# A batched matmul of fp32 inputs: releasing the first of sixteen output stores one load earlier

## The chip, the cores and the metric

The kernel runs on one core of a Trainium2 chip. The metric is the device time of one execution in microseconds (us), as the median of several runs. The times inside an execution come from one profiled execution of each kernel. In the profile PE is TensorE, PEld its weight loads, DVE is VectorE, ACT ScalarE, POOL GpSimd, SP SyncE; a trailing q (SPq) is that engine's sequencer.

## The reference

```python
# batch, m, k, n = 16, 512, 512, 512; a and b are float32
def reference(a, b):
    return np.matmul(a, b.transpose(0, 2, 1)).astype(np.float32)
```

The inputs are 33.55 MB and the output is 16.78 MB, so 50.33 MB cross between memory and the core's on-chip buffer.

## The kernel before

The work goes in eight pairs of matrices. Pair u is fed by load 2u (two matrices of a, 2.10 MB) and load 2u+1 (two of b), and it makes outputs 2u and 2u+1, each stored by one transfer of 1.05 MB. VectorE casts each load to bf16, TensorE transposes it and multiplies, ScalarE copies transposed a's and the results out of PSUM, the memory that TensorE writes. Seven slots hold loads (NL) and seven hold outputs (NO). All loads but one and the last eight stores are issued by SyncE into one queue; the first eight stores are issued by GpSimd into another one. A store in GpSimd's queue can therefore share the transfer engines with the loads; a store in SyncE's queue stands behind all the loads that were issued before it (store 8, issued by SyncE at 73.36 us, landed at 104.66, after load 15 at 99.49).

```python
NL = 7
NO = 7
STORES = "SSSSOSOSOSSOOOOOO"               # GpSimd: S issues a store, O frees an output slot
LATE = {11: (8, 9), 13: (10, 11), 15: (12, 13)}   # SyncE: stores issued after load n landed
# ... (buffers, semaphores)

def load(n, engine=nc.sync):
    u, slot = n // 2, n % NL
    # ... (source address)
    if n >= NL:
        nc.sync.wait_ge(s_cd, n - NL + 2)          # the slot has been cast
    engine.dma_start(ld[:, slot], src).then_inc(s_ld[slot], 16)

# ... (landed(n): the semaphore of store n, and 16)

def store(n):
    engine = nc.gpsimd if n < STORES.count("S") else nc.sync
    engine.wait_ge(s_out, n + 1)                   # output n is copied
    engine.dma_start(
        out[n].rearrange("(p j) n -> p j n", j=J), ob[:, n % NO]
    ).then_inc(s_st[n], 16)

load(0)
load(1, nc.scalar)
for n in range(2, NL):
    load(n)
for n in range(2 * pairs):
    nc.sync.wait_ge(s_ld[n % NL], 16 * (n // NL + 1)).then_inc(s_go, 1)
    if n > 0 and n + NL - 1 < 2 * pairs:
        load(n + NL - 1)
    for m in LATE.get(n, ()):
        store(m)
store(batch - 2)
store(batch - 1)
# ...
n_st = n_of = 0
nc.gpsimd.wait_ge(s_ld[0], 32)                     # slot 0 filled twice: load 7 has landed
for what in STORES:
    if what == "S":
        store(n_st)
        n_st += 1
    else:
        nc.gpsimd.wait_ge(*landed(n_of)).then_inc(s_of, 1)
        n_of += 1
# ... (VectorE; ScalarE takes one s_of before it writes an output, seven are given at the start;
#      TensorE)
```

## Time and profile before

| | before |
|---|---|
| time, median of the first three runs | 125.56 us (125.42 to 125.84) |
| span in the profile | 123.7 us |
| mean transfer rate over the span | 407 GB/s |
| load 7, load 15 landed | 42.26, 99.49 us |
| last store issued, landed | 113.69, 122.26 us |

The lines are shown with the prediction. Three things matter when reading them. The page's DMA row gives the busy tenths of the 16 transfer engines in 40 slices of about 3.1 us, and the GB/s row what they moved. The table by stretches counts a packet's bytes where the packet starts, so a stretch of 2 us is rough by some per cent. A line of a timeline ends, in brackets, with the idle time of the engine before it and what ended it. The landing times come from the trace's completion records: the last of 16 engines counts.

### The profile page before, as it was taken

What the parts mean: (1) busy time and instruction counts of PE and PEld (TensorE: products, weight loads), DVE (VectorE), ACT (ScalarE), POOL (GpSimd) and SP (SyncE); (2) the same over time, 40 slices, a digit from 0 to 9 for tenths busy, and PEclk for the clock granted to TensorE, in tenths of its full rate; (3) what the DMA queues carried; (4) which work ended last, traced back from release to release, by engine and by line L of the source; (5) the groups of instructions that cost most, each with busy time, mean ns of one, the idle gap of its engine ahead of it and who ended that gap; (6) DMA issues with size and microseconds to landing.
All of it is one profiled execution on the core that took longest, in us unless ns stands there. A gap on an engine that the chain in (4) does not pass through costs nothing. (4 is left out here: it accounts for less than half of the span.)

```text
span 123.7 us, 2364 instructions
## 1 busy us (share of the span) xinstructions
PE 90.8 (73%) x768; PEld 55.9 (45%) x768; DVE 68.1 (55%) x96; ACT 68.0 (55%) x130; POOL 5.2 (4%) x14
## 2 busy tenths in 40 slices
PE   0000189999999899989998999999899919995000
PEld 0000177447644754674476347645754528441000
DVE  0000698983895689289918974865957078400000
ACT  4000065478855956795589369765946069655000
POOL 2000000000000250001010110000000000000000
PEclk9999999999999999999999999999999986999955
DMA  4999999999999999999999999999999999999990
GB/s 148 413 435 429 429 429 424 429 424 435 435 424 424 429 392 363 445 416 424 453 405 437 443 408 443 424 424 458 397 445 427 408 429 427 429 427 429 424 387 8
DMA packets 4608, 50.33 MB, mean 407 GB/s; under 512 B 512, under 2 KB 512, under 8 KB 512
## 3 DMA queue, kind: packets, MB, share of 16 engines
q1 hardware_dynamic: 3312, 39.85, 76.2%
q0 software_dynamic: 1152, 8.39, 16.1%
q10 hardware_dynamic: 144, 2.10, 4.2%
HBM read 33.55 MB, written 16.78 MB: 407 GB/s over the span
## 5 line engine op out<-in xcount | busy, mean ns | idle before, releaser
L249 PE MATMUL ps<-tb,ta 128*128 128x512 bf16 x256 | 57.8, 379 | 0.5
L207 ACT COPY ob<-ps 128x512 f32 x64 | 34.4, 589 | 29.2 <-PE ps L249 21.3
L189 ACT COPY ta<-tp 128x512 bf16<-128x512 bf16 x64 | 32.9, 610 | 15.0 <-PE tp L230 15.0
L249 PEld LDWEIGHTS ps<-tb,ta 128*128 128x128 bf16 x256 | 24.1, 98 | 30.6 <-issue 4.0
L230 PE MATMUL tp<-ident,ha 128*128 128x128 bf16 x256 | 19.3, 228 | 18.1 <-PEq L135 18.1
L230 PEld LDWEIGHTS tp<-ident,ha 128*128 128x128 bf16 x256 | 16.3, 102 | 21.9 <-issue 20.1
L170 DVE COPY tb<-tp 128x1024 bf16<-128x1024 bf16 x32 | 21.2, 684 | 4.2 <-DVEq L135 4.2
L230 PE MATMUL tp<-ident,hb 128*128 128x128 bf16 x256 | 18.5, 230 | 3.4 <-PEq L135 3.4
L230 PEld LDWEIGHTS tp<-ident,hb 128*128 128x128 bf16 x256 | 16.3, 103 | 4.0 <-issue 4.0
L154 DVE CAST ha<-ld 128x1024 bf16 x8 | 5.5, 687 | 14.3 <-DVEq L135 14.3
L165 DVE COPY ha<-wa 128x2048 bf16<-128x2048 bf16 x8 | 5.5, 691 | 12.7 <-DVEq L135 12.7
L160 DVE CAST wa<-ld 128x2048 bf16 x8 | 9.8, 1220 | 0.0
L160 DVE CAST wb<-ld 128x2048 bf16 x8 | 9.7, 1217 | 0.0
L154 DVE CAST hb<-ld 128x1024 bf16 x8 | 5.5, 692 | 7.3 <-DVEq L135 7.3
L103 POOL DMA_DIRECT2D out_dram<-ob x8 | 4.5, 570 | 65.5 <-DMA ld<-in_b_dram 40.9
L169 DVE COPY hb<-wb 128x2048 bf16<-128x2048 bf16 x8 | 5.5, 685 | 0.1
L157 DVE CAST ha<-ld 128x1024 bf16 x8 | 5.5, 686 | 0.0
L157 DVE CAST hb<-ld 128x1024 bf16 x8 | 5.5, 686 | 0.0
L180 ACT ACT_TABLE_LOAD x1 | 1.3, 1283 | 1.5 <-SPq L43 1.5
L79 POOL TENSOR_SCALAR_AFFINE_SELECT ident<-ident 128x128 bf16<-128x128 bf16 x1 | 0.3, 283 | 0.2 <-POOL ident L77 0.2
L77 POOL MEMSET ident<- 128x128 bf16 x1 | 0.2, 204 | 0.5 <-SPq L43 0.5
L180 ACT COPY one<-const-float32-1.0 128x1 f32<-128x1 f32 x1 | 0.2, 192 | 0.0
(4 smaller groups left out, 0.4 us busy)
## 6 DMA issues: line engine op xcount, KB each, us to landing
ld<-in_a_dram SPq DMA_DIRECT2D x8, 2048.0 KB, 26.5
ld<-in_b_dram SPq DMA_DIRECT2D x7, 2048.0 KB, 29.6
out_dram<-ob POOLq DMA_DIRECT2D x8, 1024.0 KB, 28.9
out_dram<-ob SPq DMA_DIRECT2D x8, 1024.0 KB, 19.7
ld<-in_b_dram ACTq DMA_DIRECT2D x1, 2048.0 KB, 12.0
```

Of the source, the lines that this page charges most:

```text
L103: engine.dma_start(out[n].rearrange("(p j) n -> p j n", j=J), ob[:, n % NO]).then_inc(s_st[n], 16)
L154: nc.vector.tensor_copy(out=h[:, :J, :], in_=src[:, :J, :HK]).then_inc(s_cd, 1)
L157: nc.vector.tensor_copy(out=h[:, J:, :], in_=src[:, J:, :HK]).then_inc(s_c, 1)
L160: nc.vector.tensor_copy(out=w[:], in_=src[:, :, HK:]).then_inc(s_w, 1)
L165: nc.vector.tensor_copy(out=ha[:], in_=wa[:]).then_inc(s_ca, 1)
L169: nc.vector.tensor_copy(out=hb[:], in_=wb[:]).then_inc(s_cb, 1)
L170: nc.vector.tensor_copy(out=tb[:, ko, :], in_=tp[:, 2 + ko % 2].rearrange("k j p -> k (j p)"),).then_inc(s_eb, 1)
L180: nc.scalar.copy(out=one[:], in_=nc.const_aps.tensor(1.0, (P, 1), f32))
L189: c = nc.scalar.copy(out=ta[:, ko, e * J * P:(e + 1) * J * P].rearrange("k (j p h) -> k j p h", j=J, h=2), in_=tp[:, ko % 2, :, e * HP:(e ...
L207: c = nc.scalar.copy(out=dst[:, j, :].rearrange("m (p j) -> m p j", j=2 * J), in_=ps[:, j, :].rearrange("m (j p) -> m p j", j=2 * J),)
L230: t = nc.tensor.transpose(tp[:, 2 * x + g, j, :], h[:, j, g * P:(g + 1) * P], ident[:])
L249: t = nc.tensor.matmul(ps[:, j, :], ta[:, ko, (e * J + j) * P:(e * J + j + 1) * P], tb[:, ko, :].rearrange("k (j p) -> k j p", j=2 * J)[:, ...
```

## The change

The intent is to let the first store move one load earlier, while the three stores after it keep their old release. Numbering loads from 0, store 0 now waits for load 6 (the seventh), and store 1 and those behind it for load 7.

```diff
         n_st = n_of = 0
-        nc.gpsimd.wait_ge(s_ld[0], 32)
         for what in STORES:
+            if what == "S" and n_st == 0:
+                nc.gpsimd.wait_ge(s_ld[6], 16)
+            if what == "S" and n_st == 1:
+                nc.gpsimd.wait_ge(s_ld[0], 32)
             if what == "S":
                 store(n_st)
                 n_st += 1
```

## The prediction

> **What bounds the kernel now.** I read the page first (busy shares and slices), then the busy table by stretches of time, then the DMA queues' completion records, then the timelines of GpSimd, VectorE and ScalarE and the list of issues. The page's slices and queues first:
>
> ```profile
> PE   0000189999999899989998999999899919995000
> DMA  4999999999999999999999999999999999999990
> GB/s 148 413 435 429 429 429 424 429 424 435 435 424 424 429 392 363 445 416 424 453 405 437 443 408 443 424 424 458 397 445 427 408 429 427 429 427 429 424 387 8
> DMA packets 4608, 50.33 MB, mean 407 GB/s; under 512 B 512, under 2 KB 512, under 8 KB 512
> ...
> q1 hardware_dynamic: 3312, 39.85, 76.2%
> q0 software_dynamic: 1152, 8.39, 16.1%
> ```
>
> The DMA row is at 9 from the second slice to the last but one, also in the last 8 us where TensorE has long finished. The 16 transfer engines are the bound; TensorE runs at 9 in the middle but is not what ends. The page's chain of waits ends with ScalarE's last copy at 113.7 us and so misses the 8.6 us of stores after it. The table by stretches (us; busy us and instruction counts per engine; TensorE clock; DMA share; GB/s):
>
> ```profile
> 12.50:42.00 29.50, 25.52 (x224) 16.58 (x224) 22.42 (x32) 17.80 (x35) 0.00 (x0) 1.00 1.01 429
> 42.00:46.00 4.00, 3.47 (x39) 2.41 (x40) 3.50 (x6) 2.98 (x6) 2.32 (x4) 1.00 1.04 410
> 46.00:48.50 2.50, 2.50 (x13) 1.10 (x12) 2.50 (x5) 1.63 (x4) 0.00 (x0) 1.00 0.93 344
> 48.50:98.00 49.50, 47.21 (x405) 28.35 (x404) 33.46 (x48) 33.68 (x66) 2.21 (x4) 1.00 1.01 428
> 98.00:105.00 7.00, 4.32 (x52) 3.85 (x49) 4.92 (x7) 4.80 (x10) 0.00 (x0) 0.76 1.01 425
> ```
>
> Loads alone run at 429 GB/s, loads mixed with stores at 428, stores alone (113 to 120 us) at 428. The only loss in mid-run is where the stores begin: at 428 GB/s, 42 to 46 us lacks 4 x (1 - 410/428) = 0.17 us and 46 to 48.5 us lacks 2.5 x (1 - 344/428) = 0.49 us. The time, 125.56 us, is the span, 123.7 us, plus 1.9 us outside it.
>
> GpSimd's timeline shows the wait that the change splits (start us, us, what, idle before and its releaser):
>
> ```profile
> 42.56 2.32 POOL L103 DMA_DIRECT2D out_dram<-ob  x4 [40.88 <-DMA ld<-in_b_dram]
> 55.91 0.53 POOL L103 DMA_DIRECT2D out_dram<-ob  x1 [11.04 <-DMA out_dram<-ob]
> 63.23 0.53 POOL L103 DMA_DIRECT2D out_dram<-ob  x1 [6.78 <-DMA out_dram<-ob]
> 70.55 1.15 POOL L103 DMA_DIRECT2D out_dram<-ob  x2 [6.78 <-DMA out_dram<-ob]
> ```
>
> Counting loads from 0, load 7 landed at 42.26 us and four stores were issued at once. Their first packet moved only at 46.93 us. The completion records (last of 16 engines) then read: loads 6, 7, 8, 9, 10 at 37.36, 42.26, 47.80, 55.20, 62.51 us, loads 14 and 15 at 92.09 and 99.49; stores 0, 1, 2, 6 at 55.33, 62.65, 69.96, 99.69. A load alone takes 4.9 us (2.10 MB); a load and a store side by side 7.33 us (3.15 MB at 429 GB/s).
>
> The timelines show who waits on late loads and stores, and the list of issues (shortest, median, longest ns; first to last start) when the last store is issued:
>
> ```profile
> 84.89 0.69 DVE L154 CAST hb<-ld 128x1024 bf16 x1 [2.45 <-DVEq L135]
> 92.53 0.69 DVE L154 CAST ha<-ld 128x1024 bf16 x1 [0.83 <-DVEq L135]
> 99.82 0.69 DVE L154 CAST hb<-ld 128x1024 bf16 x1 [4.86 <-DVEq L135]
> 99.99 2.05 ACT L207 COPY ob<-ps 128x512 f32 x4 [4.82 <-ACTq L135]
> ```
>
> ```profile
> L103 SPq DMA_DIRECT2D out_dram<-ob x8: 332/332/347, 73.4 to 113.7; - x8
> ```
>
> Each cast starts 0.3 to 0.4 us after its load (13, 14, 15) landed. ScalarE at 99.99 us waited for output slot 6, freed by store 6 at 99.69. From load 15 to the last issue at 113.69 us there are 14.2 us of work. The last store landed at 122.26 us, 8.6 us after its issue, since others were queued ahead.
>
> **What the Trainium skill says.** "DMA: Bandwidth & Descriptors", section "Measured", gives 425 GB/s for a 16 MB load with the other core idle; here 429, so the rate is at its ceiling and only holes can be won. The same page, "Queues, rings and completion order", says that each engine goes round between the queues that have work. The trace agrees: from 48.5 to 98 us the 8 KB store packets of q0 and the 16 KB load packets of q1 share the bytes about 1 to 2, and a load and a store finish together every 7.33 us. The same page, "Latency and other measured facts", gives about 1 us to the first byte of a transfer issued from GpSimd; this trace shows 4.4 us (42.56 to 46.93), and the measured one is used.
>
> **The change, part by part.** It adds one wait on GpSimd (seven loads landed) and moves the old one behind store 0. No byte, no copy and no matmul is added; a semaphore wait shows no busy time.
> 1. Store 0 is issued at 37.36 + 0.3 = about 37.7 us instead of 42.56. Its data are there: pair 0's outputs were copied by 29.5 us. With the same 4.4 us its first packet moves at about 42 us, as load 7 lands, so it shares with load 8.
> 2. Load 8 takes 7.33 us plus the start-up loss instead of 5.54: it lands at 42.26 + 7.33 + 0.5 = 50.1 instead of 47.80. Loads 9 to 15 then each run beside a store, as before, so all keep the delay of 2.3 us (at most 1.05 MB / 428 GB/s = 2.45). Load 15 lands at about 101.8 instead of 99.49.
> 3. Stores 1 to 3 are issued at the old 42.6 us and follow store 0 without a gap. Store 0 lands at about 50 instead of 55.33, store 6 at about 94 instead of 99.69, store 7 with load 15. ScalarE's 4.82 us wait for the slot goes away, but pair 6 now waits 2.3 us longer for load 13.
> 4. The last pair starts 2.3 us later and its work, 14.2 us, stays: last issue at about 113.69 + 2.3 = 116.0.
> 5. When load 15 is in, exactly the eight stores of SyncE are left: 8.39 MB / 428 GB/s = 19.6 us, then about 1 us in which the last engines finish (load 15 at 98.54 to 99.49, store 15 at 120.63 to 122.26: the spread grows from 0.95 to 1.63). 101.8 + 19.6 + 0.7 = 122.1, against 122.26. The delay of the loads is paid back by one store fewer after them.
> 6. Does store 15 come in time? The engines finish store 14 between 118.17 and 119.79 us. The first SyncE load took 1.7 us from issue (0.95) to its first packet (2.67), so store 15 can move from 116.0 + 1.7 = 117.7. That leaves 0.5 us on the fastest engine, about 2 on the slowest, which sets the end. Before, it was 2.8 and 4.4.
> Sum: 0 us from the order, plus or minus the start-up hole. Central value 125.5.
>
> **The rivals.**
> (a) The hole shrinks. The load packets of 44 to 47 us took up to 996 ns instead of 611, just after four stores had been written by GpSimd within 2.3 us. Later stores, issued one or two at a time, show no such dip (432 and 437 GB/s in the stretches from 56 and 63 us). If the burst of four made the hole, a single store makes a smaller one: at most 0.66 us gained, 124.9. Against it: three still come together, and the hole may belong to the first write of all.
> (b) The hole comes twice, once for each release: plus 0.5 to 0.66 us, 126.1. Against it: at the second release stores are already flowing.
> (c) The compute tail becomes the bound: if load 15 is later than I think, or TensorE's clock falls further in the longer wait (0.76 in the stretch from 98 us), the 0.5 us of step 6 is used up. As the slowest engine has 2 us, I expect 0 to 0.5 us, 126.0 at the worst.
> (d) Freed slots help the outputs come earlier. Likely true for out 13, but the transfers are the bound and it is worth nothing at the end.
>
> **Range and chances.** The order of transfers is worth 0; (a) pulls by up to 0.6 down, (b) and (c) by as much up; runs of the kernel before spread by 0.4. So 124.9 to 126.1. A gain of 2% is 2.5 us, and all holes in mid-run are 0.66 us: 0.01. A loss of 2.5 us would need a hole four times the present one, or a tail far longer than step 6: 0.02. Within 2%: 0.97.
>
> **What would show it.** Right: GpSimd's first issue near 37.7 us with one store and the next three near 42.6; load 15's cast near 102.1 instead of 99.82; ScalarE's wait near 95 to 100 us shorter and no longer for a store; last issue near 116.0; DMA row at 9 up to the same end; span 123.3 to 124.1. Wrong: a slice under 400 GB/s after 113 us (tail), two dips instead of one (b), no dip (a), or load 15 not later, which would mean that the first store did not share with a load at all. The prediction fails if the transfers' rate in the mixed stretch changes with the order, which nothing in the trace before suggests.

## The result, and the profile after

The changed kernel takes 125.62 us (125.33 to 125.98, six runs) against 125.52 us (125.26 to 125.84, six runs) for the kernel before on the same chip. The ratio is 1.0005, with a 95% interval of 0.9982 to 1.0027: the same. A ratio here is the mean time of one kernel's runs over the mean of the other's runs in the same rounds, so it is not quite the ratio of the medians quoted beside it.

The page of the changed kernel, transfer engines in 40 slices:

```profile
PE   0000089999899899989998999999479993799100
...
DMA  3999999999999999999999999999999999999980
GB/s 116 408 445 423 434 429 429 439 423 429 429 434 423 378 434 437 410 431 418 429 434 415 423 437 429 439 418 450 413 423 447 418 415 429 429 423 423 426 360 8
```

The DMA row is as full as before and ends at the same place. The low slice has moved from the 15th and 16th (392, 363) to the 14th (378). TensorE's work ends some 2 us further to the right. The table by stretches of the changed kernel (us; busy us and counts of PE, PEld, DVE, ACT, POOL; TensorE clock; DMA share; GB/s):

```profile
37.50:42.00 4.50, 4.50 (x44) 2.85 (x42) 1.94 (x3) 3.21 (x7) 1.08 (x1) 1.00 1.01 422
42.00:46.00 4.00, 3.51 (x44) 2.41 (x41) 3.50 (x7) 3.37 (x7) 1.66 (x3) 1.00 0.97 389
46.00:48.50 2.50, 2.44 (x13) 1.13 (x13) 2.50 (x4) 1.25 (x3) 0.00 (x0) 1.00 1.04 436
48.50:98.00 49.50, 45.59 (x387) 28.37 (x386) 33.91 (x48) 33.63 (x65) 2.44 (x4) 0.97 1.01 428
98.00:105.00 7.00, 5.19 (x48) 3.17 (x46) 2.58 (x4) 4.76 (x10) 0.00 (x0) 1.00 1.00 423
```

The rate of the mixed stretch, 428 GB/s, has not changed; the loss where stores begin is now in 42 to 46 us. GpSimd's timeline shows the release split as intended, with the releaser of each part:

```profile
38.16 1.08 POOL L103 DMA_DIRECT2D out_dram<-ob  x1 [36.49 <-DMA ld<-in_a_dram]
43.07 1.66 POOL L103 DMA_DIRECT2D out_dram<-ob  x3 [3.83 <-DMA ld<-in_b_dram]
51.82 0.53 POOL L103 DMA_DIRECT2D out_dram<-ob  x1 [7.09 <-DMA out_dram<-ob]
```

VectorE's timeline, the casts that answer to loads 13 and 15, and then the list of store issues:

```profile
87.49 0.69 DVE L157 CAST hb<-ld 128x1024 bf16 x1 [4.66 <-DVEq L138]
...
102.42 0.69 DVE L157 CAST hb<-ld 128x1024 bf16 x1 [4.86 <-DVEq L138]
```

```profile
L103 SPq DMA_DIRECT2D out_dram<-ob x8: 332/338/462, 73.7 to 115.9; - x8
```

Both casts wait for their loads and start 2.6 us later than before (84.89, 99.82). ScalarE no longer waits 4.82 us for a slot before it copies output 13, but 0.69 us for TensorE:

```profile
99.33 1.07 ACT L210 COPY ob<-ps 128x512 f32 x2 [0.69 <-PE ps L252]
```

The last store is issued 2.2 us later. And yet the last store lands at 122.42 us against 122.26. The wait of the last store for its turn has shrunk from 8.57 us (issue to landing) to 6.48 us.

Numbers from the completion records, in us:

| | load 8 | load 13 | load 15 | store 0 | store 6 | last issue | last landing |
|---|---|---|---|---|---|---|---|
| before | 47.80 | 84.56 | 99.49 | 55.33 | 99.69 | 113.69 | 122.26 |
| after | 50.18 | 87.16 | 102.09 | 51.24 | 95.12 | 115.93 | 122.42 |

One of the 16 engines sets these last landings. Fifteen of them had finished the last store at 121.12 us before and at 121.06 after; the sixteenth came 1.14 and 1.36 us behind. It lagged by 1.0 to 1.6 us in all kernels whose engines did not run dry, and by 0.01 us in those where they did (e1, e3, e4, e11 below). Why one engine lags stays open.

### The profile page after: what moved, and what is told of

It is laid out like the page before. It is cut to its first block, busy times and chain, and to the rows that moved or that the text cites. A ratio compares the mean times of both kernels' runs of the same rounds, so it can differ in the third digit from the quotient of the medians.

```text
span 123.8 us, 2365 instructions
## 1 busy us (share of the span) xinstructions
PE 91.1 (74%) x768; PEld 56.2 (45%) x768; DVE 68.0 (55%) x96; ACT 68.3 (55%) x130; POOL 5.9 (5%) x14
## 5 line engine op out<-in xcount | busy, mean ns | idle before, releaser
L103 POOL DMA_DIRECT2D out_dram<-ob x8 | 5.2, 651 | 60.6 <-DMA ld<-in_a_dram 36.5
## 6 DMA issues: line engine op xcount, KB each, us to landing
ld<-in_b_dram ACTq DMA_DIRECT2D x1, 2048.0 KB, 12.5
```

Source lines behind the costliest of these rows:

```text
L103: engine.dma_start(out[n].rearrange("(p j) n -> p j n", j=J), ob[:, n % NO]).then_inc(s_st[n], 16)
```

## The experiments

The theory: the transfer engines are never idle, so moving a store ahead of a load moves the load back and leaves the end where it was. This holds as long as the last output is ready before the engines run out of other stores. The rivals: the start-up loss depends on how the stores are released (as a burst, one by one, cold or warm), the compute tail takes over, or the order is worth nothing at any distance. In each experiment a store's release, its queue or the queue's first use is changed, and only e9 needs another edit for it (ScalarE's loop is split); all results were correct. The experiments ran on three chips, each beside the kernel before in the same rounds: ratios are taken within a chip, landing times are compared across them.

### e1_no_release: no release wait at all

```diff
-        nc.gpsimd.wait_ge(s_ld[0], 32)
```

> The kernel before without any release wait: a store goes as soon as its output is copied. Theory (the transfer engines are the bound, the order of transfers is worth nothing): store 0 is issued near 25 us and moves near 29, but still only eight stores share with loads, so load 15 lands at about 102 us as in the changed kernel, the last store is issued near 116 us and the time is 125.5 us (125.0 to 126.1). Rival (the loads' delay reaches the tail): the earlier the stores, the later the end; 127 us or more.

Measured: 126.19 us (126.12 to 126.41) against 125.61 of the kernel before, ratio 1.0046 (1.0029 to 1.0062). This is slightly above the range that I gave. Load 15 landed at 102.36 us as expected, but the last store was issued at 119.0 us, not near 116. VectorE's timeline shows why (the first line is the first cast of load 13, the second the first cast of load 15):

```profile
92.88 0.69 DVE L153 CAST hb<-ld 128x1024 bf16 x1 [4.52 <-DVEq L134]
...
102.95 0.68 DVE L153 CAST hb<-ld 128x1024 bf16 x1
```

The cast of load 13 starts at 92.88 us, 5.4 us later than in the changed kernel; load 15's cast then finds its data waiting, with no idle time before it. Stores that start at 32 us had all moved by 92 us, so they delayed loads 6 to 13 more than load 15. Pair 6 was late, and pair 7 queued behind it on the engines. The stretches near the end show the transfer engines running dry:

```profile
105.00:113.00 8.00, 7.45 (x81) 5.09 (x80) 4.16 (x7) 6.11 (x13) 0.00 (x0) 1.00 1.02 428
113.00:117.00 4.00, 4.00 (x21) 1.80 (x19) 0.00 (x0) 2.72 (x6) 0.00 (x0) 1.00 0.61 256
117.00:120.00 3.00, 1.19 (x6) 0.34 (x4) 0.00 (x0) 1.38 (x3) 0.00 (x0) 1.00 0.84 347
```

The share falls to 0.61 and 0.84, so the tail did become the bound here. The store issued at 119.0 us landed at 123.18, 4.18 us later, with nothing ahead of it.

### e10_at_six: all stores released when six loads have landed

```diff
-        nc.gpsimd.wait_ge(s_ld[0], 32)
+        nc.gpsimd.wait_ge(s_ld[5], 16)
```

> The kernel before with all stores released when six loads have landed (near 33 us), between no release at all (126.2 us, last issue 119.0) and the changed kernel (last issue 115.9). Theory: the end is the later of the transfer bound (landing near 122.3 us) and the last issue plus 4.15 us. Earlier sharing makes loads 12 and 13 later, so pair 6 is later and pair 7 queues behind it: last issue 116 to 118.2, so still hidden, time 125.4 to 126.0.

Measured: 125.86 us against 125.63, ratio 1.0019 (1.0005 to 1.0033). Load 13 landed at 89.80 us, load 15 at 102.42, the last issue was at 116.27 and the last landing at 122.85. The last issue is where the theory put it, with no hole at the end. The extra time over the kernel before is at the last engines: the first engine finished the last store at 120.58 us (120.63 before), the last one at 122.85 (122.26). As a mean over the 16 engines it is 120.92 us (120.85), so a few late engines make the difference. Why they lagged further here stays open.

### e2_all_at_seven: the change without its second wait

```diff
-        nc.gpsimd.wait_ge(s_ld[0], 32)
+        nc.gpsimd.wait_ge(s_ld[6], 16)
```

> All four first stores are released when seven loads have landed: the change without its second wait. Theory: as the changed kernel, 125.6 us (125.2 to 126.0), first packet near 42 us, one dip of about 0.4 to 0.7 us. Rival (the burst of four makes the hole, the single store a smaller one): the dip is clearly deeper than the changed kernel's, and the time 0.2 to 0.4 us above it.

Measured: 125.75 us against 125.61, ratio 1.0013 (1.0000 to 1.0025). Not the whole burst of four came together: store 3 waited for its output until 41.60 us. The first packet moved at 42.35 us, and the dip, reckoned as below, was 0.46 us against 0.36 in the changed kernel. So the second wait of the change does nothing that these runs can separate from zero.

### e3_at_ten and e4_at_twelve: the release moved two and four loads later

```diff
-        nc.gpsimd.wait_ge(s_ld[0], 32)
+        nc.gpsimd.wait_ge(s_ld[2], 32)      # e3; e4: s_ld[4], 32
```

> The release moved two loads later than in the kernel before (ten landed). Theory: loads 8 to 15 land sooner (load 15 near 94 us), the missing stores are paid after them, but output slots come free late and the last pair is held by them: last issue near 117 to 118 us, time 125.5 to 126.8. Rival (later stores are better since loads are what compute waits for): below 125.2 us.

> Release when twelve loads have landed. Theory: the order is free only within limits; here output 7 waits some 13 us for slot 0 (store 0 lands near 74 us), every later output is chained to a store, the last issue is near 122 us or later, the DMA row shows holes, time 128 to 133 us. Rival (order is worth nothing at any distance): 125.5 us.

Measured: e3 128.77 us (ratio 1.0263, 1.0216 to 1.0309), e4 133.30 us (ratio 1.0616, 1.0598 to 1.0634), both against 125.61. The direction was right in both, the size was missed in e3 by 2 us and in e4 by 0.3. In e3 load 13 had landed at 79.92 us and load 15 at 94.54, earlier than in the kernels before and after the change, but the outputs had no slots. ScalarE's and TensorE's timelines of e3:

```profile
94.89 2.05 ACT L207 COPY ob<-ps 128x512 f32 x4 [4.85 <-ACTq L135]
96.80 4.06 ACT L189 COPY ta<-tp 128x512 bf16<-128x512 bf16 x8
```

```profile
100.85 8.28 PE L249 MATMUL ps<-tb,ta 128*128 128x512 bf16 x32
```

Output 11 waited 4.85 us for store 4, which landed at 94.59 us. The copies of pair 6's transposed a's stand behind it in ScalarE's program, and pair 6's matmuls begin only at 100.85 us. I had expected the last pair to be held by late slots, near 117 to 118 us, and forgot that an engine's in-order program passes a wait on to the next pair. The last issue came at 121.44 us and landed 4.17 us later, after a stretch from 117 to 120 us in which nothing moved. In e4 output 7 had already waited 14 us for store 0 (ScalarE's timeline of e4):

```profile
74.89 2.05 ACT L207 COPY ob<-ps 128x512 f32 x4 [14.15 <-ACTq L135]
```

So the order is free only within limits: a store may go earlier or later as long as its slot is free when ScalarE needs it.

### e5_nine_gpsimd and e6_ten_gpsimd: more stores beside the loads

Both edits are made on the changed kernel.

```diff
-    STORES = "SSSSOSOSOSSOOOOOO"
+    STORES = "SSSSOSOSOSSOOSOOOO"       # e6: "SSSSOSOSOSSOOSSOOOO"
-    LATE = {11: (8, 9), 13: (10, 11), 15: (12, 13)}
+    LATE = {11: (9,), 13: (10, 11), 15: (12, 13)}   # e6: without the 11
```

> The changed kernel with store 8 moved from SyncE's queue (behind all loads) to GpSimd's (beside the loads): one store more shares with loads if it gets there in time. Theory (the delay of the loads is one store's bytes each, and the tail has about 0.5 us of room on the fastest engine and 2 us on the slowest): load 15 lands near 104.5 us, last issue near 118.4, last landing about 123.5 to 124.5, time 126.5 to 128. Rival (tail never matters, the transfers just go in another order): 125.6 us.

> As before with stores 8 and 9 moved to GpSimd's queue. Theory: load 15 lands near 107 us, last issue near 121, time 129 to 131, that is about 2.4 us more than with nine. Rival: 125.6 us.

Measured: 125.71 and 125.72 us against 125.47, ratios 1.0013 (0.9988 to 1.0038) and 1.0010 (0.9987 to 1.0034). My expectation was wrong: load 15 landed at 102.17 and 102.32 us, as in the changed kernel, not near 104.5 and 107. GpSimd's timeline of e5 shows that store 8 was issued in good time:

```profile
80.97 0.53 POOL L103 DMA_DIRECT2D out_dram<-ob  x1 [13.52 <-DMA out_dram<-ob]
```

It landed at 107.51 us, after all loads. A load and a store share the engines about 2 to 1 in bytes, one store to one load (7.3 us for the two). From load 8 on there are eight loads, so eight stores fit beside them, and the ninth stands behind store 7 until the loads are gone. The delay of load 15 is set by the smaller of two counts: the stores in GpSimd's queue and the loads left when they begin.

### e11_no_release_ten: early and ten

Both edits of e1 and e6 together, on the kernel before.

> No release wait, and stores 8 and 9 in GpSimd's queue too. With the first stores early there are loads left for the ninth and tenth store to share with, which was not so in the runs with nine and ten. Theory: load 15 lands near 107 us instead of 102.4, last issue near 121.4, last landing 4.15 us after it, near 125.5, time 128.0 to 129.4. Rival (the number of stores beside the loads is worth nothing, as the runs with nine and ten seemed to say): 126.2 us.

Measured: 129.09 us against 125.63, ratio 1.0292 (1.0262 to 1.0322). Load 15 landed at 107.33 us. The casts of loads 13 and 15, the end stretches and the issues of this kernel:

```profile
93.15 0.69 DVE L153 CAST hb<-ld 128x1024 bf16 x1 [4.86 <-DVEq L134]
...
107.66 0.69 DVE L153 CAST hb<-ld 128x1024 bf16 x1 [4.53 <-DVEq L134]
```

```profile
113.00:117.00 4.00, 3.94 (x23) 1.71 (x21) 1.23 (x2) 2.15 (x5) 0.00 (x0) 1.00 0.64 268
117.00:120.00 3.00, 3.00 (x16) 1.34 (x14) 0.00 (x0) 1.77 (x4) 0.00 (x0) 1.00 0.11 44
```

Now load 15's cast waits for its data, and between 117 and 120 us the engines move 44 GB/s while TensorE finishes the last pair. The last issue was at 121.17 us and its landing at 125.36, 4.19 us later. With loads left to share, two stores more beside the loads do cost what the theory said.

### What follows for the tail

The last issue can be worked out in two terms, each taken from one of these runs: load 15's landing plus 13.84 us (115.93 - 102.09 in the changed kernel), or load 13's landing plus 26.45 us (119.0 - 92.55 in e1, where it contains TensorE's slow stretch, see below), whichever is later. For e10 the terms give 116.26 and 116.25; measured 116.27. For e11 they give 121.17 and 119.27; measured 121.17. For e7 they give 116.12 and 114.82; measured 116.13.

In other kernels they come out too early: by 1.2 us in e2 (115.45; measured 116.61), 1.1 in e5, and 0.2 to 0.4 in e6, e8, e9 and the kernel before. What sets these apart in the traces is when TensorE's granted clock was low. By the trace's clock records each of these kernels has one stretch of 3.4 us in which half the clock was granted. The rows PEclk of the pages before, after and of e2, in 40 slices (the drop in the last two slices comes when TensorE has finished):

```profile
PEclk9999999999999999999999999999999986999955
PEclk9999999999999999999999999999977999999965
PEclk9999999999999999999999999999999999599975
```

In the changed kernel, e7, e10 and e11 the stretch begins at 91.0 to 96.0 us, before load 15 has landed, and load 15 to the last issue takes 13.84 or 13.85 us. In the kernel before it begins at 101.0 us, in e6, e8 and e9 at 101.4 to 104.0, and in e2 and e5 at 105.3 and 105.9: all inside the last pair's work, which then takes 14.02 to 14.21 us, and 15.00 and 14.97 in e2 and e5. In e2 two of the last pair's groups of 16 transposes took 1.87 and 1.90 us; in the changed kernel all took 1.05 or 1.06. What sets the moment of the stretch stays open.

In four kernels whose engines had run dry (e1, e3, e4, e11) the last landing came 4.17 to 4.19 us after the last issue. So the room that the last output has is estimated as its time from issue to landing less 4.18 us: 8.57 - 4.18 = 4.4 us before, 6.48 - 4.18 = 2.3 us after the change, and only 5.59 - 4.18 = 1.4 us in e2, where the slow stretch came late.

### e7_mid_load, e8_warm_queue and e9_scalar_first: the start-up loss

The loss where stores begin is estimated from the trace with each packet's bytes spread over its own duration, over ten us from the first store's issue, against 429 GB/s: 0.69 us before, 0.36 after. These are single profiles. Three kernels ask what makes it, and what the 4 us before the first packet are.

```diff
# e7, on the changed kernel: store 0 released by the fifth first-half cast
-                nc.gpsimd.wait_ge(s_ld[6], 16)
+                nc.gpsimd.wait_ge(s_cd, 5)
```

```diff
# e8, on the changed kernel: the queue is used once at the start
# ... a buffer `warm` and a semaphore `s_warm` are added
         n_st = n_of = 0
+        nc.gpsimd.dma_start(warm[:], a[0, 0:P, 0:128]).then_inc(s_warm, 16)
+        nc.gpsimd.wait_ge(s_warm, 16)
```

```diff
# e9, on the kernel before: ScalarE issues store 0 on its own queue after two pairs
-        n_st = n_of = 0
-        nc.gpsimd.wait_ge(s_ld[0], 32)
-        for what in STORES:
+        n_st, n_of = 1, 0
+        nc.gpsimd.wait_ge(s_ld[1], 32)
+        for what in STORES[1:]:
# ... ScalarE's loop split in two: pairs 0 and 1, then
+        nc.scalar.wait_ge(s_out, 1)
+        nc.scalar.dma_start(
+            out[0].rearrange("(p j) n -> p j n", j=J), ob[:, 0]
+        ).then_inc(s_st[0], 16)
# ... then pairs 2 to 7
```

> The changed kernel, but store 0 is released by the fifth first-half cast (near 34.7 us), in the middle of load 6, not at a load's landing. Question: why 3.9 to 4.4 us pass between the issue and the first packet. If it is a fixed start-up time of this queue: first packet 38.7 to 39.3 us, inside load 7. If the store waits behind the loads already handed to the engines: at a load's end, 37 or 42 us. Time 125.6 us either way (125.2 to 126.1).

> The changed kernel with a 64 KB transfer issued by GpSimd at the start into a scratch buffer. If the dip of 0.4 us where the stores begin and the 4 us before the first packet come from the first use of that queue, both go away: first packet within 2 us of the issue, no slice below 410 GB/s near 42 us, time 0.2 to 0.4 us lower. If they come from the first write to memory or from the queue's order: nothing changes, 125.6 us plus at most 0.2 for the added bytes.

> Store 0 is issued by ScalarE on its own hardware queue after pair 1's outputs (near 41 us); GpSimd's stores 1 to 3 are released when nine loads have landed (near 50 us). Question: to what the loss where the stores begin belongs (0.36 to 0.69 us in the kernels so far; load packets turn slow about 2 us after GpSimd's first issue, before the first store packet moves). If to GpSimd's issuing: no slow load packets between 41 and 48 us, first packet within 2 us of the issue, and the loss comes about 2 to 4 us after GpSimd's first issue. If to the first write to memory: the loss is near 42 us, and none follows GpSimd's issue. If both: two losses. Time 125.3 to 125.9 in all cases, since not more than 0.7 us is at stake.

Measured, e7: 125.87 us against 125.47, ratio 1.0018 (0.9995 to 1.0042). The store was issued at 35.30 us and its first packet moved at 40.02, 4.7 us later and inside load 7, which ran from about 37 to 44 us. The store did not wait for a load's end. Over all kernels with GpSimd's first store the time from issue to first packet was 3.9 to 4.7 us, so it is a start-up time beside running loads, longer and less fixed than I had set it (3.9 to 4.4).

Measured, e8: 126.11 us against 125.47, ratio 1.0043 (1.0023 to 1.0062). The small transfer, issued at 1.91 us, moved its first packet at 6.14. The first store afterwards again took 4.2 us to its first packet and lost 0.38 us. So neither comes from the first use of the queue; this first use was a load, so a first store is not ruled out. The kernel is 0.4% slower than before; its loads begin to land 0.2 to 0.3 us later than in the changed kernel, and I did not look for the rest.

Measured, e9: 125.59 us against 125.63, ratio 1.0003 (0.9989 to 1.0017). Two queues start to store in this kernel at two times, and its table by stretches (columns as above) tells them apart. ScalarE issued store 0 at 41.01 us, and its first packet moved at 44.71. GpSimd issued its first store at 49.74 us, and its first packet moved at 54.18:

```profile
41.00:43.00 2.00, 1.69 (x31) 1.55 (x29) 1.25 (x3) 1.91 (x5) 0.00 (x0) 1.00 1.02 434
43.00:45.00 2.00, 1.63 (x30) 1.48 (x28) 1.31 (x4) 2.00 (x6) 0.00 (x0) 1.00 0.94 328
45.00:47.00 2.00, 1.94 (x13) 0.78 (x11) 2.00 (x4) 0.60 (x3) 0.00 (x0) 1.00 0.96 373
...
50.00:53.00 3.00, 3.00 (x26) 1.78 (x25) 0.90 (x1) 2.03 (x4) 2.07 (x3) 1.00 1.02 437
53.00:55.00 2.00, 1.70 (x29) 1.43 (x26) 1.54 (x3) 2.00 (x5) 0.80 (x1) 1.00 1.01 426
55.00:57.00 2.00, 1.81 (x27) 1.56 (x27) 1.50 (x3) 2.00 (x5) 0.00 (x0) 1.00 1.05 446
```

The rate falls to 328 and 373 GB/s two to six us after ScalarE's issue, and it does not fall at all two to seven us after GpSimd's. Reckoned as above, 0.54 us are lost in the ten us from ScalarE's issue and 0.01 in the ten us from GpSimd's. So in this one profile the loss goes with the first store of the execution, and neither with GpSimd's issuing nor with the burst. Not shown is whether it needs the first store, or only a store that comes while loads alone are running: when GpSimd issued, store 0 was still moving, until 52.88 us. Why the load packets slow down (the first one over 750 ns comes 1.4 to 3.0 us after the issue), before the first store packet is seen to move, stays open. Its size varied from 0.15 us (e3) to 0.76 us (e10) in single profiles, and these runs give no rule for it.

None of the eleven kernels is faster than the kernel before: its engines move bytes at 428 to 429 GB/s from 12.5 us on, but for the loss at the first store, so there is little left to win by order.

## Why the prediction was right

The time was forecast at 125.5 us and measured at 125.62; within 2% was given 0.97. Step by step:

1. **Issue and first packet of store 0.** Forecast 37.7 and about 42 us; measured 38.16 and 42.44. Load 6 landed at 37.86 us in this execution instead of 37.36, as the last of its engines was further behind the first, from load 0 on (0.93 us there; 0.49 before).
2. **Delay of the loads.** Forecast load 8 at 50.1 and load 15 at 101.8 us; measured 50.18 and 102.09. The delay of load 15, 2.60 us, is a little more than the 2.45 us named as the most; the landing of the last engine includes the wider spread between engines (1.77 us instead of 0.95). As a mean over the 16 engines load 15 came 2.11 us later. e5 and e6 showed that one store shares with one load, as the step assumed, though I drew the opposite from it when I set their expectation.
3. **Earlier stores.** Forecast stores 0 and 6 at about 50 and 94 us; measured 51.24 and 95.12. ScalarE's wait of 4.82 us for a slot is gone, and, as forecast, the time did not gain by it: e6, without this wait, took 14.21 us from load 15 to the last issue, the kernel before 14.20, with TensorE's slow stretch alike in both. e3 and e4 showed what it is worth when the stores go later instead.
4. **Last issue.** Forecast 116.0 us, measured 115.93. That it agrees so closely is luck: load 15 was 0.3 us later than forecast, and the work after it took 13.84 us instead of the 14.2 that the step took over from the kernel before. There the stretch at half clock had fallen into this work; in the changed kernel it came earlier. With the stretch as late as in e2, the last issue would be near 102.09 + 15.00 = 117.1 us (an estimate), still inside the room.
5. **The payback.** Forecast last landing 122.1 us, measured 122.42, before 122.26. This is the heart of it: 2.2 to 2.6 us of delay through the whole second half were paid back at the end, since one store fewer stood there. It is shown by the completion records, not only argued; as a mean over the 16 engines the last store landed at 120.80 us against 120.85.
6. **The room of the tail.** Forecast 0.5 us on the fastest engine and about 2 us on the slowest; from the experiments 2.3 us in this trace. The tail did become the bound in e1 and e11, where the last issue was 3.1 and 5.2 us later than in the changed kernel.

Of the rivals, (a), a smaller hole from a smaller burst, failed as a mechanism: e7 and e1, which also issue a single store first, lost 0.65 and 0.59 us, and in e9 the burst lost nothing. That the changed kernel's one profile shows 0.36 us instead of 0.69 did not appear in the time. (b), two holes, did not occur: at 43.07 us the second release finds stores already flowing. (c), the tail, lay 2.3 us away; the lower clock that it feared did come late in the last pair in e2 and e5 (half of it, for 3.4 us); it went with a last issue 1.1 to 1.2 us later, which stayed inside the room.

## What to carry to other kernels

When the transfer engines are full from end to end, reordering transfers only trades early work for late work; ask not what the moved transfer gains, but whether the engines will run dry anywhere, and count that room on the last output. Here the room was 4.4 us in the profiled execution, the change spent 2.1 us of it unseen, and two further steps in the same direction (e1, e11) made the kernel 0.5% and 2.9% slower. Before relying on such room, look at every hand-over that the moved transfer feeds, slots and in-order programs included, and not only at the last load, and leave a margin for the granted clock: about 1.1 us of the room hung on when it fell.

## What the Trainium skill lacked or had wrong

- "DMA: Bandwidth & Descriptors", section "Latency and other measured facts", gives about 0.6 us to the first byte of a transfer issued by SyncE or ScalarE and about 1 us for GpSimd. Beside running loads these runs show 3.7 us (ScalarE, e9) and 3.9 to 4.7 us (GpSimd's first store); at the start of the kernel 1.0 to 1.1 us (ScalarE) and 1.7 to 2.0 us (SyncE), each from issue to first packet.
- No page names the loss at the first store of an execution while loads run: load packets of 16 KB took up to 996 ns instead of 611 in the kernel before, and 0.15 to 0.76 us were lost once, at GpSimd's first store or, in e9, at ScalarE's.
- "DMA: Bandwidth & Descriptors", section "Queues, rings and completion order", says that engines go round between queues. It does not say what follows for the share: with 16 KB packets on one queue and 8 KB packets on the other, bytes went 2 to 1, one 2.10 MB load with one 1.05 MB store in 7.3 us.
- No page gives a measured Trainium2 rate for stores from the on-chip buffer to memory, or for loads and stores together: 428 GB/s here for each, beside 429 for loads alone.
